# Four feature tiles token-major at the start of the MLPs and the short convolution, in products of 512 columns

## Chip, core and metric

The kernel runs on one core of a Trainium2 chip. The metric is the device time of one execution in microseconds (us). A core has TensorE (PE in the profile, with PEld for its weight loads), VectorE (DVE), ScalarE (ACT), GpSimd (POOL), SyncE (SP, which issues the loads here), an on-chip memory (SBUF) and the accumulators of TensorE (PSUM, eight banks of 512 fp32 columns).

## What is computed

Two blocks of two layers each, on 256 tokens of 1024 features, all in fp32. Each layer has a mixer (two kinds of attention in block 1; a difference attention and a short convolution in block 2) and an MLP of 2816 features. The parts that the change touches, cut from the reference:

```python
# block 1, each layer
h = modulate(rmsnorm(x, g_ffn_pre[i]), sh_f, sc_f)
gate = jnp.einsum('bsd,df->bsf', h, w_ffn_gate[i])
up = jnp.einsum('bsd,df->bsf', h, w_ffn_up[i])
gate = causal_depthwise_conv(gate, w_conv[i], b_conv[i])   # width 3, along the tokens
y = jnp.einsum('bsf,fd->bsd', jax.nn.silu(gate) * up, w_ffn_down[i])
x = x + gt_f[:, None, :] * rmsnorm(y, g_ffn_post[i])
...
# block 2, each layer
g, u = jnp.split(h @ w_gate_up, 2, axis=-1)
return (jax.nn.silu(g) * u) @ w_down
...
# block 2, second mixer
b_gate, c_gate, u = jnp.split(h @ w_in, 3, axis=-1)
return (b_gate * dwconv(c_gate * u, conv_w)) @ w_out
```

## The kernel before

Every fp32 operand of a large product is split into two parts, H and L (`split`, L601: ACT casts H, DVE subtracts to get L), and each product is three matmuls, HH, HL and LH (`mm3`, L611). Weights come in chunks of 1 MB, 128 rows by 2048 columns, loaded in the order of use by SP (`chunk`, L594) and split in two halves of 1024 columns (`Stream.take`, L577): tiles wh and wl. At most 24 wh and wl tiles are alive at a time, that is six chunks, and three unsplit chunks (the SLOTS entry K8).

A stage ends with `tail` (L905): for token tile 0 and then 1 (128 tokens each) it takes the sums acc, updates x, normalises it (tile u), transposes it on PE (tps), scales and shifts it (hf) and splits it into h, feature-major (h0h, h0l for the first four feature tiles, h1h, h1l for the last four). So a token tile's h is complete before the other's.

Five stages start with `first_tiles` (L872): the four MLPs (`ffn`, L1180) and the short convolution (L1488). For the first EARLY = 2 feature tiles it makes both products (gate and up, or c and u) token-major: h of one token tile is the stationary operand, the 256 columns of one feature tile's two matrices are the moving one (tiles fp, in PSUM class "acc"). Token tile 0 is done first, while tile 1's h is made. ACT copies the result to SBUF (fps), and PE transposes it back to feature-major into a bank of class "mm" (fpt). The other 20 tiles of an MLP (6 of the convolution) are made feature-major by `project_t` (L897), with weights stationary and all 256 tokens moving, straight into an "mm" bank (gu; cu and bb in the convolution).

What follows is the same for both kinds: in block 1, t (ACT) and two more steps of t (DVE) make the convolution along the tokens, then s (Silu, ACT), y = s * up (DVE), and y's split into yh (ACT) and yl (DVE). In block 2 s is made straight from the bank. y is the last reader of a tile's bank. PE adds y times w_down to the four sums acc of 512 columns. There are four banks of class "acc" and four of class "mm", each class handed out in turn (L1597).

The order of the instructions is not written by hand. The program is recorded (`Rec`), and a list scheduler (`schedule`, L382) with fixed costs for each operation takes, for an engine that is free, the operation that comes first in the recorded order of those whose operands and buffers are there. Each engine then runs its list strictly in that order.

```python
EARLY = 2
...
def mm3(self, out, a, b, start, stop):
    mm(out, lhsT=a[0], rhs=b[0], start=start, stop=False)
    mm(out, lhsT=a[0], rhs=b[1], start=False, stop=False)
    mm(out, lhsT=a[1], rhs=b[0], start=False, stop=stop)
...
SLOTS = {"S": 64, "K1": 14, "K2": 12, "K4": 32, "K8": 3, "acc": 4, "mm": 4}
```

Of the kernel before, what the change touches and what calls it, by code (L numbers as in the profile page):

```python
# [22 lines left out]
EARLY = 2  # feature tiles at the start of a stage that are made token-major, a token tile at a time  # L23
LASTF, LASTD = 6, 4  # last terms of a sum that run a token tile at a time (the MLPs, the difference attention)
VLAG, QPIECES, WOFROM = 4, 2, 13  # the difference attention's order: values behind weights, the first values, w_o
# [7 lines left out]
# ---------------------------------------------------------------- layout of the inputs  # L33


def vec_layout():
    """Columns of the packed feature-major vectors: name -> (first column, count)."""
# [69 lines left out]
def pack_small(a):  # L107
    """Vectors that every partition reads: lambda's four, the q and k gains and the gains of the
    rotation's partner features."""
# [9 lines left out]
def pack_consts():  # L119
    """Constants of the shapes alone: identity, the two causal masks, head selectors, rope tables."""  # L120
# [18 lines left out]
def pack_chunks(a, plan):  # L139
    out = np.empty((len(plan), P, CH), np.float32)  # L140
    for i, parts in enumerate(plan):
        o = 0
        for name, layer, r0, nr, c0, nc_ in parts:
            w = a[name][layer]
            if r0 is None:  # nr tiles of columns from c0, as rows
# [9 lines left out]
# ---------------------------------------------------------------- recording and ordering of the program  # L155
#
# The program is traced into operations on virtual tiles, list-scheduled on a model of the engines (first
# the operation that comes first in the trace, of those whose operands are there), and emitted in that order.
# [4 lines left out]
AGAIN = {"PE": 0.0, "DVE": 127.0, "ACT": 153.0, "POOL": 100.0, "SP": 0.0}  # from a result to its reader  # L163
# [18 lines left out]
class VAP:  # L182
    """A view of a virtual tile: the partitions, the positions on the free axes, and how to get it from the tile."""
# [79 lines left out]
class Rec:  # L263
    """Takes the place of nc and of the tile pools while the program is traced."""
# [18 lines left out]
    def record(self, eng, fn, args, kw):  # L283
# [16 lines left out]
        if fn == "matmul" and kw["start"]:  # one open group of sums in a bank  # L300
            v = outs[0]
            for w in v.t.writes:
                if w[3] is not op and w[1] < v.parts[1] and w[2] > v.parts[0]:
                    op.deps.setdefault(w[3], 1)
# [31 lines left out]
    def cost(self, op, outs, ins, args, kw):  # L336
        fn = op.fn
        n = int(outs[0].idx.size) if outs else 0
        if op.eng == "PE":
# [4 lines left out]
            side = {32: 4, 64: 2}.get(kw["lhsT"].shape[1], 1)  # tiles of columns that run side by side  # L344
# [1289 lines left out]
```

## Time and profile before

| | |
|---|---|
| time, three runs | 1366.46, 1366.72, 1367.65 us (median 1366.72) |
| span of the profiled execution, first to last instruction | 1366.3 us; no time is on record for what lies around it in that execution, and the median of the runs is 0.4 us above the span |
| busy | PE 1328.7 us (97%), DVE 1082.2 (79%), ACT 718.3 (53%), POOL 112.2 (8%) |
| mean granted TensorE clock | 0.993 |
| matmuls | 8872, each with its weight load |

Matmuls overlap, so the duration of one (0.28 us for 256 columns, 0.39 for 512) is longer than the distance from its start to the next start; the pace is read from start times. Every instruction is put down to L543, since one helper emits them all; operations are told apart by the tiles that they write and read (out<-in). "<-" behind an idle time names what ended it. The four MLPs start at about 154, 482, 876 and 1171 us, the short convolution at about 1070 us (first fp products).

### The profile page before, as it was taken

The numbers are of one execution on the slowest core, as the hardware profiler recorded it, in microseconds if no ns is written. First come the engines' busy times: TensorE is split into PE (matmuls) and PEld (weight loads), VectorE is DVE, ScalarE is ACT, GpSimd is POOL, SyncE is SP. The second block draws the span as 40 slices with busy tenths as digits, with TensorE's granted clock in tenths as the row PEclk, the third lists the DMA queues.
The fourth block names the chain that finished last, engine by engine and source line by source line (L and its number), as shares of the span: only waits on it lengthen the run. The fifth ranks groups of instructions, "written<-read, shape, count | busy, mean of one in ns | idle before, by whom it ended". The sixth has DMA issues, their size and how long they took to land.

```text
span 1366.3 us, 22283 instructions
## 1 busy us (share of the span) xinstructions
PE 1328.7 (97%) x8872; PEld 1193.9 (87%) x8872; DVE 1082.2 (79%) x1807; ACT 718.3 (53%) x1273; POOL 112.2 (8%) x168
## 2 busy tenths in 40 slices
PE   5899999999999999999999999999999999899998
PEld 3788799999888799999888888799999899899997
DVE  6888988998988499999799977877777898755542
ACT  3565665555666474557444566754444535644430
POOL 1000200000200010101143122300000100100000
PEclk9999999999999999999999999999999999999999
DMA  9857578887676156777554541577776688355520
GB/s 360 307 213 272 192 296 324 316 325 304 228 248 262 48 186 272 277 251 261 194 185 167 189 150 63 185 270 291 274 278 254 235 304 313 140 200 185 185 94 31
DMA packets 45320, 311.84 MB, mean 228 GB/s; under 512 B 5280, under 2 KB 5664, under 8 KB 8864
## 3 DMA queue, kind: packets, MB, share of 16 engines
q1 hardware_dynamic: 45216, 310.42, 61.3%
q8 instruction: 69, 1.13, 0.3%
q14 instruction: 35, 0.29, 0.1%
HBM read 309.35 MB, written 1.05 MB: 227 GB/s over the span
## 4 chain that ended last, share of the span: by engine, by line
PE 89%; DVE 4%; ACT 2%; POOL 2%; issue 2%; DMA 0%; SPq 0%; POOLq 0%; ACTq 0%
PE gu L543 34%; PE acc L543 29%; PE qkps L543 7%; PE fp L543 4%; PE cu L543 3%; PE z L543 2%; PE dz L543 2%; PE bb L543 2%; PE qps L543 2%; PE op L543 1%; DVE w L543 1%; ACT junk L543 1%; POOL sst L543 1%; PE kc L543 1%; DVE u L543 1%
## 5 line engine op out<-in xcount | busy, mean ns | idle before, releaser
L543 DVE TENSOR_TENSOR wl<-w,wh 128x1024 fp32r<-128x1024 f32 x392 | 471.3, 1220 | 82.8 <-ACT wh L543 59.7
L543 ACT CAST wh<-w 128x1024 fp32r<-128x1024 f32 x392 | 402.7, 1049 | 98.2 <-DMA w<-in_wst_dram 67.8
L543 DVE CUSTOM_DVE_ANT_0 w<-w,rows,vec 128x1024 f32<-128x1024 f32 x192 | 242.3, 1278 | 15.3 <-DMA w<-in_wst_dram 15.1
L543 PE MATMUL gu<-h1h,wl 128*128 128x256 f32 x640 | 181.4, 284 | 0.0
L543 PE MATMUL gu<-h1h,wh 128*128 128x256 f32 x640 | 181.3, 283 | 0.0
L543 PE MATMUL gu<-h0l,wh 128*128 128x256 f32 x640 | 181.3, 283 | 0.0
L543 PE MATMUL gu<-h1l,wh 128*128 128x256 f32 x640 | 181.3, 283 | 0.0
L543 PE MATMUL gu<-h0h,wl 128*128 128x256 f32 x640 | 181.3, 283 | 0.0
L543 PE MATMUL gu<-h0h,wh 128*128 128x256 f32 x640 | 181.2, 283 | 0.0
L543 PE MATMUL acc<-wh,yh 128*128 128x512 f32 x352 | 137.8, 392 | 0.7 <-ACT yh L543 0.7
L543 PE MATMUL acc<-wl,yh 128*128 128x512 f32 x352 | 137.7, 392 | 0.0
L543 PE MATMUL acc<-wh,yl 128*128 128x512 f32 x352 | 136.1, 389 | 0.0
L543 PEld LDWEIGHTS gu<-h0h,wh 128*128 128x128 f32 x640 | 122.6, 192 | 2.3
L543 PEld LDWEIGHTS gu<-h0l,wh 128*128 128x128 f32 x640 | 122.7, 192 | 2.2
L543 PEld LDWEIGHTS gu<-h1h,wh 128*128 128x128 f32 x640 | 123.0, 192 | 0.1
L543 PEld LDWEIGHTS gu<-h1l,wh 128*128 128x128 f32 x640 | 122.9, 192 | 0.0
L543 PEld LDWEIGHTS gu<-h1h,wl 128*128 128x128 f32 x640 | 122.9, 192 | 0.0
L543 PEld LDWEIGHTS gu<-h0h,wl 128*128 128x128 f32 x640 | 122.7, 192 | 0.1
L543 DVE TENSOR_TENSOR y<-s,gu 128x256 f32<-128x256 f32 x80 | 33.4, 418 | 73.1 <-ACT s L543 73.1
L543 ACT ACTIVATE s<-gu 128x256 f32<-128x256 f32 x40 | 15.4, 384 | 136.5 <-PE gu L543 136.5
L543 POOL TENSOR_SCALAR sst<-ss 128x1 f32<-128x1 f32 x26 | 25.7, 987 | 734.5 <-ACT junk L543 734.2
L543 PEld LDWEIGHTS acc<-wh,yl 128*128 128x128 f32 x352 | 66.1, 188 | 14.2
(358 smaller groups left out, 2834.1 us busy)
## 6 DMA issues: line engine op xcount, KB each, us to landing
w<-in_wst_dram SPq DMA_DIRECT2D x284, 1024.0 KB, 4.8
w<-in_wst_dram SPq DMA_DIRECT2D x16, 512.0 KB, 11.4
x<-in_x_dram SPq DMA_DIRECT2D x2, 512.0 KB, 6.5
cx<-in_ctx_dram SPq DMA_DIRECT2D x2, 512.0 KB, 6.0
out_dram<-x SPq DMA_DIRECT2D x1, 512.0 KB, 2.6
out_dram<-x SPq DMA_DIRECT2D x2, 256.0 KB, 2.0
cst<-in_consts_dram SPq DMA_DIRECT2D x1, 264.0 KB, 5.1
smalls<-in_smalls_dram SPq DMA_DIRECT2D x1, 256.0 KB, 6.7
```

The source lines that it names most:

```text
L543: fn(*[real(a) for a in op.args], **{k: real(v) for k, v in op.kw.items()})
```

## The change

EARLY goes from 2 to 4. The early tiles are made two at a time: the chunks of a pair hold, for each row tile, the columns of both tiles' two matrices side by side (512 columns), two chunks to a pair (`pair_specs` in place of `both_spec`). `first_tiles` takes the chunks of both pairs first, then makes for each token tile and pair one bank fp of 512 columns with 24 products of 512, and copies it. The transposes are as before, for four tiles. The remaining 18 tiles of an MLP (4 of the convolution, whose bb tiles are unchanged) stay feature-major. The number of chunks is unchanged. Comments and docstrings are removed as well, which changes line numbers alone.

```diff
-EARLY = 2
+EARLY = 4
...
     @staticmethod
-    def both_spec(a, b):
-        return tuple((n, i, k * P, 1, c, P) for k in range(KT) for n, i, c in (a, b))
+    def pair_specs(tiles):
+        return [
+            tuple((n, i, k * P, 1, c, P) for k in range(g * 4, g * 4 + 4) for t in tiles for n, i, c in t) for g in range(2)
+        ]
 
     def first_tiles(self, ht, n):
         nc = self.nc
-        ws = [self.w.take() for f in range(n)]
+        ws = [sum((self.w.take() for g in range(2)), []) for p in range(n // 2)]
         out = {}
         for t in range(2):
-            for f in range(n):
-                if f % 2 == 0:
-                    ps = self.pacc.tile([P, 512], F32, tag="acc", name="fp")
-                    out[t, f // 2] = self.sb.tile([P, 512], F32, name="fps")
-                o = f % 2 * S
+            for p in range(n // 2):
+                ps = self.pacc.tile([P, 512], F32, tag="acc", name="fp")
                 for kt in range(KT):
-                    w = [z[:, kt % 4 * S : (kt % 4 + 1) * S] for z in ws[f][kt // 4]]
-                    self.mm3(ps[:, o : o + S], self.hx(ht, t, kt), w, kt == 0, kt == KT - 1)
-                if f % 2 == 1 or f == n - 1:
-                    nc.scalar.copy(out[t, f // 2][:, 0 : o + S], ps[:, 0 : o + S])
+                    w = [z[:, kt % 2 * 512 : (kt % 2 + 1) * 512] for z in ws[p][kt // 2]]
+                    self.mm3(ps, self.hx(ht, t, kt), w, kt == 0, kt == KT - 1)
+                out[t, p] = self.sb.tile([P, 512], F32, name="fps")
+                nc.scalar.copy(out[t, p], ps)
...
         tiles = [[(n, i, c + f * P) for n, c in ab] for f in range(NF)]
-        return [self.both_spec(*x) if f < EARLY else tuple((n, i, 0, 8, c, P) for n, i, c in x) for f, x in enumerate(tiles)]
+        out = []
+        for f in range(0, EARLY, 2):
+            out += self.pair_specs(tiles[f : f + 2])
+        return out + [tuple((n, i, 0, 8, c, P) for n, i, c in x) for x in tiles[EARLY:]]
...
-        out = [self.both_spec(cols(1, f), cols(2, f)) for f in range(EARLY)]
+        out = []
+        for f in range(0, EARLY, 2):
+            out += self.pair_specs([(cols(1, f + k), cols(2, f + k)) for k in range(2)])
```

The scheduler makes a new order of it. The first place is PE in the first MLP, behind the last token-major products of token tile 1 (fp_1688 before). fpt_1714 and fpt_1718 are the transposed tiles 0 and 1, gu_1777 and gu_1856 the products of tiles 2 and 3; "waits" names whose progress the instruction waits for. Before:

```order
L543 MATMUL fp_1688<-wh_1612,h1h_1587 128x256
L543 MATMUL fp_1688<-wl_1622,h1h_1587 128x256
L543 MATMUL fp_1688<-wh_1612,h1l_1594 128x256
L543 MATMUL gu_1777<-h0h_1569,wh_1709 128x256 [waits Activation_49]
L543 MATMUL gu_1777<-h0l_1577,wh_1709 128x256
L543 MATMUL gu_1777<-h0h_1569,wl_1725 128x256 [waits DVE_49]
```

And now, where fp_1758 is token tile 1's second pair, fpt_1805, 1810, 1819 and 1824 are the transposed tiles 0 to 3, and gu_1858 is tile 4:

```order
L543 MATMUL fp_1758<-wh_1699,h1l_1593 128x512
L543 MATMUL fpt_1805<-eye_85,fps_1706 128x128 [waits Activation_49]
L543 MATMUL fpt_1805<-eye_85,fps_1762 128x128 [waits Activation_49]
...
L543 MATMUL fpt_1810<-eye_85,fps_1762 128x128
L543 MATMUL fpt_1819<-eye_85,fps_1735 128x128 x2
L543 MATMUL fpt_1824<-eye_85,fps_1735 128x128 x2
L543 MATMUL fpt_1819<-eye_85,fps_1812 128x128 [waits Activation_49]
L543 MATMUL fpt_1819<-eye_85,fps_1812 128x128
L543 MATMUL fpt_1824<-eye_85,fps_1812 128x128 x2
L543 MATMUL gu_1858<-h0h_1569,wh_1767 128x256 [waits DVE_49]
```

Where gu products followed the token-major ones before, all sixteen transposes follow now. gu_1858 is the fifth tile in the four "mm" banks from fpt_1805 on, and the DVE step that it waits for is y_1850, of tile 0.

The second place is DVE in the same MLP, the steps between the last subtractions of weights and y. Before (t_365 and t_380 are tiles 0 and 1):

```order
L543 TENSOR_TENSOR wl_1803<-w_400_1712,wh_1787 128x1024 [waits DMAHW0_49,Activation_49]
L543 SCALAR_TENSOR_TENSOR t_365_1799<-fpt_1714,vec_90,t_365_1799 128x255 [waits Activation_49]
L543 SCALAR_TENSOR_TENSOR t_365_1799<-fpt_1714,vec_90,t_365_1799 128x254 [waits DVE_49]
L543 SCALAR_TENSOR_TENSOR t_380_1808<-fpt_1718,vec_90,t_380_1808 128x255 [waits Activation_49]
L543 SCALAR_TENSOR_TENSOR t_380_1808<-fpt_1718,vec_90,t_380_1808 128x254 [waits DVE_49]
L543 TENSOR_TENSOR wl_1840<-w_400_1712,wh_1814 128x1024 [waits Activation_49]
L543 TENSOR_TENSOR y_1854<-s_1831,fpt_1714 128x256 [waits Activation_49]
```

And now (t_379, t_394, t_400 and t_411 are tiles 0 to 3):

```order
L543 TENSOR_TENSOR wl_1800<-w_426_1743,wh_1791 128x1024 [waits DMAHW2_49,PE_49,Activation_49]
L543 TENSOR_TENSOR wl_1816<-w_426_1743,wh_1802 128x1024 [waits PE_49,Activation_49]
L543 SCALAR_TENSOR_TENSOR t_379_1822<-fpt_1805,vec_90,t_379_1822 128x255 [waits Activation_49]
L543 SCALAR_TENSOR_TENSOR t_379_1822<-fpt_1805,vec_90,t_379_1822 128x254 [waits DVE_49]
L543 SCALAR_TENSOR_TENSOR t_394_1829<-fpt_1810,vec_90,t_394_1829 128x255 [waits Activation_49]
L543 SCALAR_TENSOR_TENSOR t_394_1829<-fpt_1810,vec_90,t_394_1829 128x254 [waits DVE_49]
L543 SCALAR_TENSOR_TENSOR t_400_1834<-fpt_1819,vec_90,t_400_1834 128x255 [waits Activation_49]
L543 SCALAR_TENSOR_TENSOR t_400_1834<-fpt_1819,vec_90,t_400_1834 128x254 [waits DVE_49]
L543 SCALAR_TENSOR_TENSOR t_411_1839<-fpt_1824,vec_90,t_411_1839 128x255 [waits Activation_49]
L543 TENSOR_TENSOR y_1850<-s_1842,fpt_1805 128x256 [waits Activation_49]
```

Seven steps of t stand ahead of the first y, four of them before. On ACT the last copy fps, the four t, the load of the Silu table and three s follow each other in that order, where before two t, a cast, the table load and two s did. In the second MLP the three engines have the same order there; in the third there are no t, and the table load stands between the last copy and the first s; in the fourth no table is loaded. In the short convolution the 48 products bb of tiles 0 and 1 stand between the transposes of tiles 1 and 2.

## Rows read from the trace of the kernel before

**Rows 1.** The page: busy time of each engine, and the shares of the chain that ended last, by engine.

```profile
PE 1328.7 (97%) x8872; PEld 1193.9 (87%) x8872; DVE 1082.2 (79%) x1807; ACT 718.3 (53%) x1273; POOL 112.2 (8%) x168
...
PE 89%; DVE 4%; ACT 2%; POOL 2%; issue 2%; DMA 0%; SPq 0%; POOLq 0%; ACTq 0%
```

**Rows 2.** Who waited for whom, PE's waits: waiting tile and what it waited for, us in total, times, longest.

```profile
PE tps L543 <- DVE u L543: 6.1, 6, 2.7
PE fp L543 <- ACT h0h L543: 4.2, 8, 0.8
...
PE fpt L543 <- ACT fps L543: 0.3, 1, 0.3
```

**Rows 3.** PE's timeline in the middle of the first MLP: start us, us, engine, line, operation, shape. Between the first two rows stand 47 more products of 256 columns (gu), between the last two 11 more of 512 (acc).

```profile
199.92 0.28 PE L543 MATMUL gu<-h0h,wh 128*128 128x256 f32 x1
...
205.67 0.40 PE L543 MATMUL acc<-wh,yh 128*128 128x512 f32 x1
...
208.42 0.28 PE L543 MATMUL gu<-h0h,wh 128*128 128x256 f32 x1
```

**Rows 4.** PE's timeline at the end of the first MLP's token-major products: the first gu product, the four transposes of a tile, the product behind them.

```profile
171.26 0.28 PE L543 MATMUL gu<-h0h,wh 128*128 128x256 f32 x1
...
172.34 0.60 PE L543 MATMUL fpt<-eye,fps 128*128 128x128 f32 x4
172.70 0.36 PE L543 MATMUL gu<-h0h,wh 128*128 128x256 f32 x1
```

**Rows 5.** PE's timeline, rows with idle time ahead of them (in brackets, with what ended it) at the starts of the first, second and third MLP and of the short convolution.

```profile
152.65 1.06 PE L543 MATMUL tps<-eye,u 128*128 128x128 f32 x8 [1.73 <-DVE u L543]
...
165.16 0.39 PE L543 MATMUL fp<-wh,h0h 128*128 128x256 f32 x1 [0.33 <-ACT h0h L543]
...
165.95 0.66 PE L543 MATMUL fpt<-eye,fps 128*128 128x128 f32 x4 [0.28 <-ACT fps L543]
...
491.59 0.39 PE L543 MATMUL fp<-wh,h0h 128*128 128x256 f32 x1 [0.31 <-ACT h0h L543]
...
883.40 1.06 PE L543 MATMUL tps<-eye,u 128*128 128x128 f32 x8 [0.52 <-DVE u L543]
...
1071.11 0.38 PE L543 MATMUL fp<-wh,h0h 128*128 128x256 f32 x1 [0.24 <-ACT h0h L543]
...
1071.85 0.39 PE L543 MATMUL fp<-wh,h0l 128*128 128x256 f32 x1 [0.24 <-DVE h0l L543]
...
1076.34 1.09 PE L543 MATMUL tps<-eye,u 128*128 128x128 f32 x8 [0.16 <-DVE u L543]
...
1078.59 0.39 PE L543 MATMUL fp<-wh,h0h 128*128 128x256 f32 x1 [0.45 <-ACT h0h L543]
```

**Rows 6.** Timeline of ACT, then of DVE, from the last copy fps of the first MLP to the first y.

```profile
171.46 0.59 ACT L543 COPY fps<-fp 128x512 f32<-128x512 f32 x1 [1.76 <-PE fp L543]
171.94 1.05 ACT L543 CAST wh<-w 128x1024 fp32r<-128x1024 f32 x1
172.89 1.02 ACT L543 ACTIVATE t<-fpt,vec 128x256 f32<-128x256 f32 x2
...
175.24 1.28 ACT L543 ACT_TABLE_LOAD   x1 [0.39 <-DVE t L543]
176.53 0.73 ACT L543 ACTIVATE s<-t 128x256 f32<-128x256 f32 x2
...
174.17 1.90 DVE L543 SCALAR_TENSOR_TENSOR t<-fpt,vec,t 128x255 f32<-128x255 f32 x4
...
177.12 0.74 DVE L543 TENSOR_TENSOR y<-s,fpt 128x256 f32<-128x256 f32 x2
```

**Rows 7.** ACT's timeline at the same place of the third MLP.

```profile
893.80 0.58 ACT L543 COPY fps<-fp 128x512 f32<-128x512 f32 x1 [0.51 <-PE fp L543]
894.40 1.28 ACT L543 ACT_TABLE_LOAD   x1
895.93 0.66 ACT L543 ACTIVATE s<-fpt 128x256 f32<-128x256 f32 x2 [0.25 <-PE fpt L543]
```

**Rows 8.** Stretches: from and to, length, then busy us (and instructions) of PE, PEld, DVE, ACT and POOL, the granted TensorE clock, the DMA share, GB/s.

```profile
30.90:34.30 3.40, 1.74 (x8) 1.12 (x6) 3.40 (x8) 1.05 (x1) 0.00 (x0) 1.00 1.02 408
34.30:37.70 3.40, 2.44 (x11) 2.03 (x12) 3.40 (x6) 1.94 (x4) 0.00 (x0) 1.00 1.05 426
...
147.00:153.80 6.80, 4.99 (x26) 3.78 (x24) 6.53 (x11) 4.91 (x12) 4.05 (x7) 1.00 0.52 195
153.80:160.60 6.80, 6.15 (x28) 6.07 (x29) 5.97 (x13) 6.80 (x16) 3.48 (x3) 0.50 0.22 94
...
874.00:877.40 3.40, 1.91 (x12) 1.44 (x13) 3.31 (x10) 2.20 (x8) 0.06 (x1) 1.00 0.86 308
877.40:880.80 3.40, 3.40 (x18) 3.36 (x17) 3.40 (x7) 3.40 (x10) 1.80 (x1) 0.50 0.01 2
...
1167.60:1171.00 3.40, 1.24 (x9) 1.03 (x10) 2.94 (x9) 1.85 (x7) 1.07 (x3) 1.00 0.00 0
1171.00:1174.40 3.40, 3.38 (x14) 3.00 (x15) 2.94 (x8) 3.23 (x8) 2.68 (x1) 0.50 0.00 0
```

**Rows 9.** Groups of instructions on ACT and on DVE, the split of weights: count, busy us and mean ns of one, idle time before them and what ended it.

```profile
L543 ACT CAST wh<-w 128x1024 fp32r<-128x1024 f32 x392 | 402.7, 1049 | 98.2 <-DMA w<-in_wst_dram 67.8 <-PE gu L543 17.7 <-PE acc L543 5.4
L543 DVE TENSOR_TENSOR wl<-w,wh 128x1024 fp32r<-128x1024 f32 x392 | 471.3, 1220 | 82.8 <-ACT wh L543 59.7 <-PE gu L543 11.5 <-issue 10.5
```

## The prediction

> **What bounds the kernel now.** I read the page first: PE is busy for 1328.7 of the 1366.3 us span, and 89% of the chain that ended last lies on PE [rows 1]. So time is won or lost only where PE does its products at another pace or stands idle. Next I read PE's waits by releaser. Apart from the load phase at the start, the entries that touch this change are the waits of the transposes for u, of the first products for h, and a short one for their copy: 6.1, 4.2 and 0.3 us [rows 2]. The reader should see that almost nothing is idle in the middle of a stage. The trace before shows no wait of the first gu product for a bank.
>
> Then I read PE's timeline for the pace, because the durations of overlapping products say nothing about it. From 199.92 to 205.67 us, 48 products of 256 columns start, 0.1198 us apart; the next 12, of 512 columns, take 2.75 us, 0.2292 us apart [rows 3]. Four transposes stand 0.36 us before the next product, so one is 0.09 us [rows 4].
>
> **The change, part by part.** All sums are made against the profiled execution, whose span is 1366.3 us. The median of the runs shown is 1366.72 us, so I add 0.4 us at the end.
>
> *Products.* In each of five stages (four MLPs, the short convolution) the first four feature tiles took 96 token-major products of 256 columns for tiles 0 and 1 and 96 feature-major ones of 256 for tiles 2 and 3: 192 x 0.1198 = 23.0 us. Now they are 96 products of 512: 96 x 0.2292 = 22.0 us. That is -1.0 us a stage and -5.0 us in all. The Trainium skill, "TensorE: Matmul & The Clock Gate", section Back-to-back issue gap, gives a fixed cost of 2.5 ns for each product on top of its columns; by that 96 fewer products would save 0.24 us a stage, 1.2 us in all, and the forecast would be 3.8 us later. The rows decide, and they show 10.4 ns for each pair of products made one.
>
> *Transposes.* Tiles 2 and 3 now have to be turned too: 8 more in a stage, 8 x 0.09 = 0.72 us, in all +3.6 us, on PE and hidden by nothing. The two more copies from PSUM a stage lie on ACT (53% busy) beside PE's work; the last of them is in the chain below.
>
> *Weights.* The number of chunks is unchanged, and so are their loads, casts and subtractions (1049 and 1220 ns each [rows 9]). Four chunks instead of two must be split when a stage starts, but token tile 0 also has 48 x 0.2292 = 11.0 us of products in place of 5.75, and PE's new order puts products of token tile 1 with the first pair wherever the second pair's halves are due. I cost this at nothing; without that cover it is one subtraction, 1.2 us, for each stage.
>
> *Waits that go.* Inside the starts PE waited for token tile 1's h, or for its transposes' input, or for the copy: 0.33 and 0.28 us in the first MLP, 0.31 in the second, 0.52 in the third, and 0.24, 0.24, 0.16 and 0.45 in the convolution, 2.5 us together [rows 5]. A piece of h now feeds three products of 0.2292, 0.69 us in place of 0.36, and a second pair can fill in, so most go: I take -2.0 us (bounds 0 and -2.5). The wait for token tile 0 (1.73 us at 152.65 [rows 5]) stays: nothing new can run before the first h.
>
> *The new wait.* The transposed tiles go to the four "mm" banks. Before, tiles 0 and 1 took two and the gu products of tiles 2 and 3 used the others, so PE had 96 products to do while ACT and DVE worked on tiles 0 and 1. Now four transposed tiles fill all four banks, and the first gu product (tile 4) waits on DVE: for y of tile 0, the last reader of its bank. Behind it on PE stand all of gu and the first acc products; nothing overtakes. The length, with T the moment at which PE goes from the products to the transposes: the copy starts 0.20 us after T (171.26 to 171.46 [rows 4, 6]) and takes 0.59, to 0.79. PE does its 16 transposes meanwhile and, at T + 1.5, is out of work. In the first two MLPs the chain on ACT and DVE is: t of tile 0 from 0.68 (the step from copy to next is 0.48) for 0.56, to 1.24; then on DVE seven steps of t before y, 0.475 each (four in 1.90 us), from about 1.4 to 4.7. Meanwhile ACT does the other three t at steps of 0.46, to 2.6, loads its table (1.28), to 3.9, and makes s (0.42), to 4.3 [rows 6]. So y runs from 4.7 to 5.1, and PE goes on at about 5.3. That is an idle stretch of 3.8; I take 3.7 us, twice. In the third MLP there is no convolution, but there is the table load: copy to 0.79, table to 2.1, s 0.36 to 2.5, y to 3.1 [rows 6, 7], PE at 3.2: 1.7 us. In the fourth no table is loaded: s to 1.2, y to 1.8, PE at 1.9: 0.4 us. In the short convolution the bb products stand between the transposes of tiles 1 and 2 and take the third bank at once: 0. Together +9.5 us (bounds 6 if every hand-over is as short as it can be, 12 if DVE still has one subtraction to do ahead of the t steps).
>
> *The clock.* Where PE stood idle at a stage start, the granted clock fell to 0.50, 1.2 GHz, soon after: it was busy 4.99 of 6.80 us before the fall at 153.8 (6.8 us long), 1.91 of 3.40 before the one at 877.4, and 1.24 of 3.40 before the one at 1171; but with 1.74 of 3.40 at 30.9 it stayed at 1.00 [rows 8]. A fall of 3.4 us costs 1.7 us of products. The two waits of 3.7 us, with 1.5 us of short transposes ahead of them, are as idle as the stretch at 1167.6, so I expect a fall after each: +3.4 us. The wait of 1.7 us is like the one at 874, as likely to bring a fall as not; I leave it out of the sum and in the range. The Trainium skill, same page, section A second HAM failure mode: psum-queue depth-cycling, says that cycling through PSUM banks makes PE idle briefly between groups of products so often that its clock goes back and forth. This speaks against the change; the trace agrees as far as it shows a fall after short idle stretches, and shows none yet that a bank caused.
>
> The sum: -5.0 + 3.6 - 2.0 + 9.5 + 3.4 = +9.5 us; 1366.3 + 9.5 + 0.4 = **1376.2 us**.
>
> **The rivals.**
> - *The waits come, the clock holds*: +6.1 us, 1372.8. For it: the stretch at 30.9, idle for half of its time without a fall. Against it: the falls after three of the five tails. If the waits are at their lower bound too, it is 1369.3.
> - *The second pair's weights are late* as well: 1.2 us for each of five stages, 1382. For it: ACT and DVE do their splitting in order with the tail, and the wait for the copy at 165.95 shows that ACT is full there. Against it: PE's order fills these places with other products.
> - *The wider products win*, the other side: the banks come free in time because the chain from copy to y is passed faster than its rows say, and what is left is -5.0 + 3.6 - 2.0 = -3.4 us, 1363.3. The place is the first gu product of each MLP; it decides for faster from an average wait below 0.85 us (3.4 over four stages), with no fall of the clock. For it: before, the same chain never held PE up. Against it: then gu products covered it, and the table load alone is 1.28 us.
> - *The change doesn't do what it says* (the 512-column products run at the pace of two of 256): the sum is 5.0 us later, 1381.2. The acc rows, with the same shape and the same kind of operands, speak against it.
>
> **How the numbers follow.** Forecast 0.58; clock holds 0.19; late weights 0.09; wider products win 0.09; no gain in pace 0.05. What a measurement of this kernel can tell from no change is about 0.2%, 2.7 us: faster is below 1364.0, slower above 1369.4. Faster has 0.05 (half of its rival), within 0.2% 0.09 (the other half, and the lowest part of the case in which the clock holds), slower 0.86. The range goes from 1369 (short waits, clock held) to 1382 (a third fall, or a second stretch at half clock as at 153.8, with no wait gone); the forecast's own is 1374 to 1379.
>
> **What would show it.** In PE's waits a new entry, gu on DVE y, four times: about 3.7, 3.7, 1.7 and 0.4 us. The fp products still 480, but of 512 columns and 0.229 us apart, gu 576 a group in place of 640, and 80 transposes fpt in place of 40. In the clock's rows two stretches at 0.50 soon after the first gu product of the first two MLPs. On ACT the table load after four t, with PE idle beside it. I am wrong if PE's timeline shows no idle time ahead of gu, if that idle time is under 1 us, or if fp waits for weights (wh, wl) for more than 2 us in all.

## The result, and the profile after

The changed kernel takes 1375.18 us (median of four runs) where the kernel before takes 1366.72 beside it (median of three): the ratio is 1.006, with a 95% interval from 1.0048 to 1.0072. It is slower, 8.5 us by the medians, and 1 us below the 1376.2 that was predicted. One more run of the kernel before (1839 us) and the profiled run of acc_banks below (1845 us) fell into a much slower state of the chip, and no figure of this document uses them. The profiled execution took 1374.88 us with a span of 1373.1, which is 6.8 us more than the span before. In the runs on record the time is 1.7 to 2.2 us above the span, so the profiled execution before, with its span of 1366.3, was itself some 1.3 us above its median, and the spans differ by less than the medians.

The page of the changed kernel, busy time and the chain by engine, against [rows 1]:

```profile
PE 1326.3 (97%) x8432; PEld 1169.1 (85%) x8432; DVE 1083.3 (79%) x1807; ACT 724.1 (53%) x1283; POOL 110.1 (8%) x168
...
PE 81%; DVE 9%; ACT 3%; POOL 3%; issue 2%; DMA 2%; SPq 0%; POOLq 0%; ACTq 0%; DVEq 0%
```

PE's busy time hardly moved. The chain tells more: PE's share went from 89% to 81%, DVE's from 4% to 9%. The same work now more often waits for DVE. PE's waits (waiting tile, what it waited for, us in total, times, longest), against [rows 2]:

```profile
PE gu L543 <- DVE y L543: 7.8, 4, 3.1
...
PE tps L543 <- DVE u L543: 7.1, 7, 2.5
...
PE fp L543 <- ACT h0h L543: 3.2, 5, 0.8
PE acc L543 <- ACT yh L543: 2.8, 3, 1.4
...
PE fp L543 <- DVE wl L543: 0.5, 1, 0.5
```

The first entry is the new wait that was predicted. The entry of acc was not: before, acc waited once for yh, 0.7 us; now it waits three times, 2.8 us. The timelines at the end of the first MLP's token-major products (start, us, engine, operation, shape, idle time before; compare [rows 4, 6]). PE's:

```profile
177.22 0.39 PE L543 MATMUL fp<-wh,h1l 128*128 128x512 f32 x1
177.45 1.91 PE L543 MATMUL fpt<-eye,fps 128*128 128x128 f32 x16
182.43 0.58 PE L543 MATMUL gu<-h0h,wh 128*128 128x256 f32 x1 [3.08 <-DVE y L543]
```

ACT's, from the last copy to s:

```profile
177.70 0.59 ACT L543 COPY fps<-fp 128x512 f32<-128x512 f32 x1 [1.12 <-PE fp L543]
178.18 2.01 ACT L543 ACTIVATE t<-fpt,vec 128x256 f32<-128x256 f32 x4
180.21 1.28 ACT L543 ACT_TABLE_LOAD   x1
181.51 1.03 ACT L543 ACTIVATE s<-t 128x256 f32<-128x256 f32 x3
```

DVE's, the t steps and y:

```profile
178.79 3.21 DVE L543 SCALAR_TENSOR_TENSOR t<-fpt,vec,t 128x255 f32<-128x255 f32 x7 [0.39 <-ACT t L543]
181.96 1.08 DVE L543 TENSOR_TENSOR y<-s,fpt 128x256 f32<-128x256 f32 x3
```

From the first transpose to the first gu product pass 4.98 us; the prediction's chain gave 5.3. The table load and the seven t steps run side by side, and y starts at 181.96, when both s (0.42 after 181.51) and the t steps have just ended.

Where the time came from is best seen by stage, each from its first fp product in PE's timeline to the next stage's (the last to PE's last instruction), in us:

| stretch | before | after |
|---|---|---|
| start to first MLP | 154.4 | 152.7 |
| first MLP and second attention | 327.6 | 330.0 |
| second MLP and difference attention | 394.4 | 403.3 |
| third MLP | 193.1 | 192.2 |
| short convolution | 101.2 | 100.0 |
| fourth MLP | 190.5 | 189.9 |

Three stretches with the change are faster, and most of the loss is in that of the second MLP: 8.9 us, of which the new wait is 3.1. The clock has a part in the others: before, 6.8 us of the first MLP and 3.4 of the third ran at half clock [rows 8], and in the changed kernel 3.4 of the first MLP alone. That alone takes 1.7 us off each of the two stretches, more than the whole gain of the third MLP. The second MLP's stretch has no half clock in either kernel. The 1.7 us ahead of the first MLP need not be the change's: before_rows below, whose edit stands behind that place, takes 153.0 there.

### The profile page after: what moved, and what is told of

Its sections match the earlier page's. It is cut to its first block, busy times and chain, and to the rows that moved or that the text cites. A ratio compares the mean times of both kernels' runs of the same rounds, so it can differ in the third digit from the quotient of the medians.

```text
span 1373.1 us, 21420 instructions
## 1 busy us (share of the span) xinstructions
PE 1326.3 (97%) x8432; PEld 1169.1 (85%) x8432; DVE 1083.3 (79%) x1807; ACT 724.1 (53%) x1283; POOL 110.1 (8%) x168
## 4 chain that ended last, share of the span: by engine, by line
PE 81%; DVE 9%; ACT 3%; POOL 3%; issue 2%; DMA 2%; SPq 0%; POOLq 0%; ACTq 0%; DVEq 0%
PE gu L543 27%; PE acc L543 27%; PE qkps L543 7%; PE fp L543 6%; DVE w L543 3%; PE z L543 2%; DVE wl L543 2%; PE dz L543 2%; PE cu L543 2%; PE qps L543 2%; DMA w<-in_wst_dram 1%; PE op L543 1%; DVE djunk L543 1%; PE bb L543 1%; POOL sst L543 1%
## 5 line engine op out<-in xcount | busy, mean ns | idle before, releaser
L543 PE MATMUL gu<-h0h,wh 128*128 128x256 f32 x576 | 164.1, 285 | 8.0 <-DVE y L543 7.8
L543 PE MATMUL gu<-h0h,wl 128*128 128x256 f32 x576 | 163.8, 284 | 0.2 <-DVE wl L543 0.2
L543 PE MATMUL gu<-h0l,wh 128*128 128x256 f32 x576 | 163.5, 284 | 0.0
L543 PE MATMUL gu<-h1h,wh 128*128 128x256 f32 x576 | 163.1, 283 | 0.0
L543 PE MATMUL gu<-h1l,wh 128*128 128x256 f32 x576 | 163.0, 283 | 0.0
L543 PE MATMUL gu<-h1h,wl 128*128 128x256 f32 x576 | 163.0, 283 | 0.0
L543 PEld LDWEIGHTS gu<-h1h,wh 128*128 128x128 f32 x576 | 110.7, 192 | 0.1
L543 PEld LDWEIGHTS gu<-h1l,wh 128*128 128x128 f32 x576 | 110.6, 192 | 0.0
L543 PEld LDWEIGHTS gu<-h1h,wl 128*128 128x128 f32 x576 | 110.5, 192 | 0.1
L543 PEld LDWEIGHTS acc<-wh,yh 128*128 128x128 f32 x352 | 66.3, 188 | 15.6 <-ACT yh L543 3.6
```

The source lines that it names most:

```text
L543: fn(*[real(a) for a in op.args], **{k: real(v) for k, v in op.kw.items()})
```

## The experiments

All times are medians, beside the kernel before on the same chip. Where kernels that stand beside different times of the kernel before are compared, the difference is good to about 1 us: its medians go from 1366.7 to 1367.9.

| kernel | time | before | ratio, 95% interval |
|---|---|---|---|
| two_wide | 1368.74 | 1367.72 | 1.0007, 0.9998 to 1.0016 |
| four_narrow | 1383.37 | 1367.72 | 1.0116, 1.0102 to 1.0130 |
| acc_banks | 1367.39 | 1367.72 | 0.9996, 0.9987 to 1.0005 |
| gu_between | 1370.76 | 1367.72 | 1.0019, 1.0010 to 1.0028 |
| after_rows | 1371.38 | 1367.62 | 1.0025, 1.0014 to 1.0036 |
| before_rows | 1366.00 | 1367.62 | 0.9991, 0.9982 to 1.0000 |
| two_wide_rows | 1361.49 | 1367.62 | 0.9958, 0.9945 to 0.9970 |
| acc_banks_rows | 1363.55 | 1367.62 | 0.9972, 0.9961 to 0.9983 |
| rows_late | 1379.09 | 1367.93 | 1.0083, 1.0070 to 1.0097 |
| silu_first | 1366.94 | 1367.93 | 0.9996, 0.9987 to 1.0004 |
| gu_between_rows | 1364.16 | 1367.93 | 0.9972, 0.9962 to 0.9983 |
| mixed_rows | 1358.75 | 1367.93 | 0.9934, 0.9921 to 0.9948 |

### Width, tiles and banks apart

**two_wide** is the changed kernel with one pair, **four_narrow** the kernel before with four tiles.

```diff
-EARLY = 4
+EARLY = 2
```

> Two early feature tiles as before, but as one pair in products of 512 columns: width alone, without the two more transposed tiles and without a full set of mm banks. My theory (the banks cost, the width gains): fp is 48 products of 512 a stage at 0.229 us in place of 96 of 256 at 0.120, so -0.5 us a stage and -2.5 us in all against the kernel before, with at most 1 us of the small waits inside the starts gone besides; no wait of gu for y; 1363.5 to 1365.5 us where the kernel before has 1367.2. Rival (width gains nothing, all that the changed kernel shows comes from the order): within 0.5 us of the kernel before. Second rival (fp of a pair needs two chunks split before it ends, and these come late): fp waits for wh or wl by 1 us or more a stage, slower than before by 3 us or more.

It came out at 1368.7, 1.0 above before: neither the gain of the width nor the rival's nothing, and no late weights (one wait of fp for wl, 0.5 us). By stage the first, third and fourth MLP, the convolution and the start took 5.0 us less than before, the second MLP with the difference attention 6.9 more, though no gu waits for a bank there at the start. The 5.0 can't be read as the width's: the 10.2 us at half clock at 153.8 and 877.4 us of the kernel before [rows 8] are not in this execution, and they alone are 5.1 us of products. The 6.9 holds, since neither kernel has half clock there. So something in the second MLP is lost without the banks.

```diff
-EARLY = 2  # feature tiles at the start of a stage that are made token-major, a token tile at a time
+EARLY = 4  # feature tiles at the start of a stage that are made token-major, a token tile at a time
```

> Four early feature tiles, but each in products of 256 columns as before: the banks and transposes of the changed kernel without its width. My theory: the new wait of gu for y stays as in the changed kernel (3.1, 3.1, 1.1 us at the starts of the first three MLPs), and the products cost 1.0 us more a stage, so 5 us more than the changed kernel: 1379 to 1381 us. Rival (the width gains nothing): 1374 to 1376. If the order around the second MLP is what costs the changed kernel most (its waits for yh and weights in the middle, 3.4 us), it can go either way by some 3 us here, and the waits of that MLP must then differ from the changed kernel's while the new waits stay.

1383.4, above the expected range: 8.2 us more than the changed kernel, 7.2 when each is set against the kernel before beside it. That is more than the 5.0 of the sum, but not the width alone: waits differ too. The new wait is 3.0, 1.5 and 1.1 us in the first three MLPs; in the second the transposes had waited 1.0 us before for ACT's copy of rows (on rows, see below), and one gu waits 1.5 us for wl. The pace of fp is read from PE's timeline in the second MLP. In four_narrow 84 products lie from the first row to the second:

```profile
499.88 0.28 PE L543 MATMUL fp<-wh,h0l 128*128 128x256 f32 x1
...
509.96 0.28 PE L543 MATMUL fp<-wh,h1l 128*128 128x256 f32 x1
```

In the changed kernel 49:

```profile
494.74 0.39 PE L543 MATMUL fp<-wl,h1h 128*128 128x512 f32 x1
...
505.84 0.39 PE L543 MATMUL fp<-wh,h1l 128*128 128x512 f32 x1
```

That is 0.1200 us against 0.2265: 13.5 ns for each pair of products made one, 1.3 us a stage, 6.5 in all.

**acc_banks** and **gu_between** both free the bank on which the first gu waits.

```diff
+            pool = self.pmm if f < 2 else self.pacc
-            ps = self.pmm.tile([P, 512], F32, tag="mm", name="fpt")
+            ps = pool.tile([P, 512], F32, tag="mm", name="fpt")
```

> The changed kernel with the transposed tiles 2 and 3 in two of the acc banks, so that two mm banks are free for the gu products of tiles 4 and 5. My theory (the banks cost): the wait of the first gu for y goes at all four MLPs (7.8 us in the changed kernel); instead the first acc product, 20 to 44 gu products later, waits for the y of tiles 2 and 3, which leave the acc banks: at most 2 us in each of the first two MLPs and nothing in the others, so 1368 to 1372 us. The fall of the clock after the first MLP's wait need not come, 1.7 us less. Rival (the wait is for the work of ACT and DVE on the four tiles and only moves to acc): the waits move to acc in full and the time stays within 1.5 us of the changed kernel's 1375.2. Second rival (the second MLP's waits for yh and weights, 3.4 us, have a cause of their own): these stay whatever the bank does.

1367.4, level with before, 7.8 below the changed kernel and 0.6 under the expected range. By the time, the wait did not move in full, and the theory of the banks holds. Its waits are not read here, so the second rival is left to the next kernel; those of the same banks with early rows stand under acc_banks_rows.

```diff
+        fs = [0, 1, 4, 5, 2, 3] + list(range(6, NF))
-        wd = Stream(self, [((name, i, f * P, 2, 0, D),) for f in range(0, NF, 2)])
+        wd = Stream(self, [((name, i, f * P, 2, 0, D),) for f in fs[::2]])
...
-        for f in range(NF + 1):
+        for n in range(NF + 1):
+            f = fs[n] if n < NF else NF
...
-            j = f - 1
+            j = fs[n - 1] if n else -1
...
-                self.bg(max(0, (f - 3) / (NF - 4)))
+                self.bg(max(0, (n - 3) / (NF - 4)))
```

> The changed kernel with the gu products of tiles 4 and 5 put, in the MLPs, between the transposes of tiles 0, 1 and those of tiles 2, 3, so that the banks are shared out as before: two transposed tiles, two of gu. My theory (the banks cost): 48 or more gu products (5.8 us) cover the chain from copy to y, the wait of gu for y goes at all four MLPs (7.8 us) and no other takes its place, so 1365.5 to 1368.5 us, the kernel before's time; without the fall of the clock after it 1.7 us less. Rival (the wait only moves, since ACT and DVE have the same four tiles to do at the start): waits of acc for yh or of fpt for banks of 1 us and more in the first two MLPs, 1371 us or more. Second rival (the waits in the middle of the second MLP have a cause of their own, DVE's background work or the weights): these stay at 2 us or more while the wait for the bank goes.

1370.8, between the theory's range and the first rival's. Its trace speaks for the second rival: no wait for the bank at an MLP's start, and in the middle of the second MLP (482 to 632 us, PE's waits) this:

```profile
PE acc L543 <- ACT yh L543: 4.4, 3, 3.0
PE gu L543 <- DVE y L543: 0.6, 1, 0.6
```

### What is lost in the second MLP

So the second MLP was read again. Stretches of the kernel before (length, then busy us of PE, PEld, DVE, ACT, POOL, the granted clock, DMA share, GB/s):

```profile
500.00:520.00 20.00, 20.00 (x137) 18.55 (x137) 19.08 (x35) 10.17 (x18) 0.00 (x0) 1.00 0.53 202
520.00:540.00 20.00, 20.00 (x148) 19.02 (x147) 19.73 (x27) 10.49 (x15) 0.00 (x0) 1.00 0.77 297
540.00:560.00 20.00, 20.00 (x140) 18.65 (x139) 18.13 (x30) 8.46 (x13) 0.00 (x0) 1.00 0.62 232
```

The same of the changed kernel:

```profile
500.00:520.00 20.00, 16.92 (x90) 14.36 (x89) 11.10 (x21) 10.87 (x19) 0.00 (x0) 1.00 0.43 157
520.00:540.00 20.00, 20.00 (x144) 18.76 (x143) 13.29 (x22) 6.41 (x12) 0.00 (x0) 1.00 0.26 97
540.00:560.00 20.00, 18.47 (x130) 16.77 (x129) 18.62 (x28) 8.57 (x12) 0.00 (x0) 1.00 0.72 275
560.00:580.00 20.00, 19.28 (x137) 17.77 (x137) 19.89 (x33) 11.63 (x22) 6.72 (x6) 1.00 0.77 286
580.00:600.00 20.00, 19.08 (x135) 17.55 (x134) 19.89 (x32) 9.69 (x14) 0.00 (x0) 1.00 0.76 290
```

Before, DVE works almost without a break from 500 us on. After, it is idle for 15.6 of the 40 us from 500 to 540, the loads fall to 97 GB/s, and then DVE is full (19.89 of 20) while PE has holes. What DVE does there beside the MLP's own steps is background work of the difference attention's modulation (djunk, w): products of loaded chunks with two tiles rows, which PE makes by 16 transposes rowps of cact into "mm" banks and ACT copies. In the kernel before, ACT's timeline has the last copies of rows here:

```profile
493.71 1.10 ACT L543 COPY rows<-rowps 128x512 f32<-128x512 f32 x2
```

and DVE's the first djunk, which waits only for its chunk:

```profile
500.15 1.28 DVE L543 CUSTOM_DVE_ANT_0 djunk<-w,rows,vec 128x1024 bf16<-128x1024 f32 x1 [0.86 <-DMA w<-in_wst_dram]
```

In the changed kernel PE's timeline has the transposes here:

```profile
527.84 1.91 PE L543 MATMUL rowps<-eye,cact 128*128 128x128 f32 x16
```

DVE's has the first djunk:

```profile
531.28 1.28 DVE L543 CUSTOM_DVE_ANT_0 djunk<-w,rows,vec 128x1024 bf16<-128x1024 f32 x1 [0.72 <-ACT rows L543]
```

and between 523 and 537 us SP's queue waited for one thing:

```profile
SPq L543 <- DVE msh_a L543: 14.4, 1, 14.4
```

Before, those transposes stood between the first token-major products of the stage, 482.7 to 491.3 us, in PE's timeline from

```profile
482.71 0.54 PE L543 MATMUL rowps<-eye,cact 128*128 128x128 f32 x3
...
490.46 0.82 PE L543 MATMUL rowps<-eye,cact 128*128 128x128 f32 x6
```

where the changed kernel has wide products. After, PE makes them at 527.8, behind the gu products of tile 4 and 48 acc products. The first two chunks of the background work were loaded all the same, at 492.5 and 501.6 us, in the order recorded. There are three buffers for unsplit chunks (K8 in SLOTS); two of them held these chunks until rows was there, so every weight chunk had to pass through the third. The next load, of the third background chunk, stood 14.4 us in SP's queue until DVE was done with the first, and the weights behind it stood too. In two_wide 12 of the 16 transposes are early, but the last copy of rows is at 526.06 us, and the first djunk at 527.5.

**after_rows, before_rows, two_wide_rows, acc_banks_rows** record the two rows tiles ahead of the second MLP, so that PE makes them first thing; nothing else differs from the kernel in their name.

```diff
+        for k in (1, 2):
+            self.cb[k] = self.on_all_rows(self.cact[:, k * 8 : k * 8 + 8])
+
         def units():
-            for k in (1, 2):
-                self.cb[k] = self.on_all_rows(self.cact[:, k * 8 : k * 8 + 8])
             yield from self.mod_units(1, 0, MODS[:2])
```

> The changed kernel with one edit: the two rows tiles (the conditions, spread over all partitions by 16 transposes into mm banks) that the second MLP's background work on DVE reads are recorded ahead of that MLP instead of inside it. My new theory: the changed kernel makes rows 40 us later than the kernel before (531 us against 490), and until then two and then all three of the unsplit-chunk buffers hold chunks of that background work, so weight loads stand (from 521.7 to 536.5 us none is issued) and DVE, idle first, is late afterwards: this, not the banks, made some 6 us of the changed kernel's 8. Then the waits for yh and weights in the middle of the second MLP (3.7 us) go, second MLP and difference attention take about 397 us in place of 403, and the time is 1368.5 to 1370.5 us. Rival (the waits there come from the bank wait having put gu and acc out of step): no change in that MLP beyond 1 us, 1374 to 1376.

1371.4, 3.8 below the changed kernel (0.9 above the expected range). In its second MLP the waits for yh and for weights are gone; the wait for the bank grew from 3.1 to 4.0, and 3.4 us at half clock follow it (the last row of this document). These two, 0.9 and 1.7 us, are why the stretch took 399.1 and not 397. PE's waits there, 482 to 632 us:

```profile
PE gu L543 <- DVE y L543: 4.0, 1, 4.0
PE fp L543 <- ACT h0h L543: 0.6, 1, 0.6
```

And DVE (the third busy time) is full again where the changed kernel's was idle:

```profile
500.00:520.00 20.00, 15.99 (x75) 13.36 (x74) 19.55 (x35) 13.04 (x21) 0.00 (x0) 0.91 0.56 201
520.00:540.00 20.00, 20.00 (x132) 18.42 (x131) 17.97 (x26) 7.78 (x11) 0.00 (x0) 1.00 0.66 247
```

> The kernel before with the same edit (rows recorded ahead of the second MLP): there PE makes rows at the start of the MLP anyhow, in gaps of 480 to 491 us. New theory: within 1 us of the kernel before, 1367 to 1368.5. Rival (making rows early is a gain of its own that has nothing to do with the change): faster than before by 2 us or more.

1366.0, a gain of 1.6 whose interval reaches to no gain: 1.0 better than expected and short of the rival's 2. The edit gives the others 3.8 to 7.2, so most of that is the late rows; up to 1.6 of it may be a gain that the edit has in any case.

> One pair of 512 columns (two early tiles) with rows recorded ahead of the second MLP. Without that edit it was 1368.7, no faster than before, though its first, third and fourth MLP and the convolution together took 5 us less in the trace and the second MLP with the difference attention 6.9 us more. New theory (late rows hid the gain of the width): the second MLP's loss goes, 1362.5 to 1365 us, faster than the kernel before by 0.2% or more. Rival (the second MLP loses because the pair itself asks for its weights in another order): 1367 us or more.

1361.5, 7.2 less than two_wide, faster than before and 1 us under the expected range. The second MLP with the difference attention takes 393.5 us in place of 401.3. The width had gained all along, and late rows had hidden it.

> Four early tiles in pairs, tiles 2 and 3 transposed into acc banks, and rows recorded ahead of the second MLP: both causes taken away. Without the second edit it was 1367.7. If the two causes add (bank waits 7.2 us, late rows some 6), 1361 to 1363.5 us, and no wait of gu for y or of acc for yh above 0.5 us in the first two MLPs. If they are the same loss seen twice (DVE and ACT have the early tiles to do in any case), 1366 to 1368.

1363.55, at the upper end: the causes add. Against after_rows the banks are worth 7.8, against acc_banks the rows 3.8. PE's waits over the first two MLPs (152 to 632 us) name no y and no yh:

```profile
PE fp L543 <- ACT h0h L543: 1.3, 2, 0.7
PE tps L543 <- DVE u L543: 0.7, 1, 0.7
PE fp L543 <- DVE wl L543: 0.6, 1, 0.6
PE acc L543 <- ACT h0h L543: 0.3, 1, 0.3
```

### The cause put in by hand, the chain, and the best of both

**rows_late** is the kernel before with one small DVE operation ahead of the rows:

```diff
+                self.lasty = y
...
+            late = self.sb.tile([P, 16], F32, name="late")
+            self.nc.vector.scalar_tensor_tensor(
+                out=late, in0=self.lasty[:, 0:16], scalar=0.0, in1=self.cact[:, 8:24], op0=ALU.mult, op1=ALU.add
+            )
             for k in (1, 2):
-                self.cb[k] = self.on_all_rows(self.cact[:, k * 8 : k * 8 + 8])
+                self.cb[k] = self.on_all_rows(late[:, k * 8 - 8 : k * 8])
```

> The kernel before, made to have its rows late: the 16 columns from which the two rows tiles are made pass first through one small DVE operation that adds zero times y of tile 4, so that PE cannot make rows before that y (some 43 us into the second MLP); bit for bit the same values, nothing else changed. My theory (chunks of the background work that wait for rows hold the unsplit-chunk buffers, so weight loads stand and DVE is late afterwards): a stretch of 10 us or more without a load between 500 and 530 us, waits of acc for yh in the middle of the second MLP, 3 to 8 us slower than the kernel before, 1370.5 to 1375.5. Rival (the second MLP loses time only when four early tiles or a pair change the order of the weights): within 1.5 us of the kernel before.

1379.1, 11.2 us slower, more than expected (3 to 8). Late rows alone, without any wide product or full set of banks, cost more than the whole change. Stretches of this kernel:

```profile
500.00:520.00 20.00, 20.00 (x137) 18.55 (x136) 10.83 (x20) 10.47 (x18) 0.00 (x0) 1.00 0.38 142
520.00:540.00 20.00, 20.00 (x149) 18.98 (x148) 10.66 (x19) 5.99 (x11) 0.00 (x0) 1.00 0.32 109
```

Its longest entry of PE's waits from 482 to 632 us:

```profile
PE acc L543 <- ACT yh L543: 4.5, 3, 1.9
```

The picture is that of the changed kernel, stronger: DVE idle for 18.5 of 40 us, the first djunk at 533.74.

**silu_first** is after_rows with the table loaded earlier.

```diff
-    def first_tiles(self, ht, n):
+    def first_tiles(self, ht, n, silu=False):
...
                 nc.scalar.copy(out[t, p], ps)
+                if silu and t == 0 and p == n // 2 - 1:
+                    first = self.sb.tile([P, 1], F32, name="first")
+                    nc.scalar.activation(out=first, in_=out[t, p][:, 0:1], func=AF.Silu)
...
-        early = self.first_tiles(self.h, EARLY)
+        early = self.first_tiles(self.h, EARLY, True)
```

> The changed kernel with rows early, and with ACT's table load for Silu moved out of the chain from copy to y: a Silu of one column of token tile 0's last copy, whose result nobody reads, loads the table 11 us earlier, beside the products of token tile 1. My theory (the wait for the bank is the length of the chain copy, t, table load, s, y): the wait of the first gu falls from 3.1 to about 1.9 us in the first MLP, from 4.0 to about 2.9 in the second (a cast stands ahead of s there), and from 1.1 to 0 in the third; 3 to 3.5 us less than without it (1371.4), 1367.5 to 1369. Rival (DVE's seven t steps alone set the end, since they end with the table load): the waits of the first two MLPs stay within 0.3 us, only the third's goes, 1370 to 1371.

1366.9, 4.4 below after_rows and a little under the range. The waits are 2.4, 2.7 and none. In the first MLP the scheduler now puts y behind four t steps in place of seven; there the wait is 0.5 longer than expected, since DVE is at a subtraction of weights until 179.3 us, 0.8 after ACT's first t. The chain sets the length of the wait, and DVE's part of it as well as ACT's.

**gu_between_rows** is gu_between with early rows.

> Four early tiles with the gu products of tiles 4 and 5 between the transposes of tiles 0, 1 and 2, 3, and rows recorded ahead of the second MLP. Without the latter it was 1370.8, with a wait of 3.0 us of acc for yh in the second MLP. If that wait was the late rows' doing: it goes with the others there, and the time is 1362 to 1365 us, like the kernel with two acc banks (1363.6). If it was the early tiles' work on ACT and DVE, moved: a wait of 2 us or more for yh or a bank stays within 50 us of the second MLP's start, 1366 to 1369.

1364.2: the wait of 3.0 for yh was late rows. **mixed_rows** takes acc_banks_rows and makes only one pair in the second, third and fourth MLP.

```diff
-        for f in range(0, EARLY, 2):
+        n = 4 if (b, i) == (0, 0) else 2
+        for f in range(0, n, 2):
...
-        early = self.first_tiles(self.h, EARLY)
+        n = 4 if (b, i) == (0, 0) else 2
+        early = self.first_tiles(self.h, n)
```

> The stages' best of the traces so far put together, with rows recorded ahead of the second MLP: four early tiles with two of them in acc banks in the first MLP and the convolution, one pair in the other three MLPs. In the traces the first MLP is 1.5 us shorter with four (325.1 against 326.6) and the convolution 1.7 us (99.1 against 100.8), the second MLP with the difference attention 3.2 us shorter with two (393.5 against 396.7) and the third MLP 1.4 (190.7 against 192.1). If stages add up: 1358 to 1360 us, below one pair in all stages (1361.5). If the loss of a stage comes with what the stage before it leaves (the wait of 4.1 us for u at the third MLP's start with four): 1361 to 1364.

1358.75: 9.2 us, 0.66%, faster than before, and the best of all kernels here. Its stretches take 152.3, 325.1, 393.5, 192.1, 99.6 and 190.7 us; the third MLP did not show the 190.7 that was counted on.

## Why the prediction was right, and where it was not

The time and the sign came out, and the new wait is of the kind and in the place that was forecast. That the number came out within 1 us is luck in part: two terms were too large and one cause was missing, and these nearly cancel. By the runs the 8.5 us are +7.8 from the banks (after_rows against acc_banks_rows), +3.8 from late rows (the changed kernel against after_rows), and -3.1 for all the rest; acc_banks_rows against the kernel before beside it gives -4.1 for that rest. The prediction had +12.9 from the banks (9.5 of waits and 3.4 of clock), nothing, and -3.4.

- **Products, -5.0.** Mis-sized: -6.5 by the pace of fp; the 7.2 to 8.2 by four_narrow hold other waits as well. The rows that were taken [rows 3] were gu and acc; fp at 512 columns is a little faster than acc (0.2265 against 0.2292). The rows show 13.5 ns for each product that falls away. The Trainium skill, "TensorE: Matmul & The Clock Gate", section Back-to-back issue gap, gives 2.5 ns, in a formula that leaves out the load of weights; with a load for each product, as here, the trace doesn't agree.
- **Transposes, +3.6.** Mis-sized. The sixteen take 1.91 us in the three MLPs where PE then waits, 1.7 in the fourth and 1.6 in the convolution, and the eight took 0.6 to 0.8 (starts in PE's timeline): +5.4 in all. The 0.09 of four transposes with a product behind them [rows 4] doesn't hold for sixteen: 0.10 each with a product behind them, 0.12 with nothing behind.
- **Weights, 0.** Right at the starts: fp waits for wl once, 0.5 us. The weights that came late were those of the second MLP's middle, and not for the reason given to the rival.
- **Waits that go, -2.0.** The step that failed. The waits inside the starts fell from 2.5 [rows 5] to 1.7 us only. And the step asked what a second pair would put into the gaps between the first products, not what stood there already: in the second MLP before, PE had made rows there, and it now makes them 40 us later. The prediction has no term for that; it is the 3.8 us of late rows.
- **The new wait, +9.5.** Right in kind and place, a little long: 3.08, 3.08, 1.09 and none, against 3.7, 3.7, 1.7 and 0.4; of the four waits that the profile counts, the fourth is another, 0.56 us later in the second MLP. The chain was 0.3 shorter than worked out, and the transposes before it 0.4 longer.
- **The clock, +3.4.** Half borne out. Stretches of the changed kernel, with the granted clock as the last but two column: the first MLP's wait and what follows, then the second's.

```profile
177.45:181.90 4.45, 1.91 (x17) 1.67 (x15) 3.95 (x8) 4.17 (x8) 0.00 (x0) 1.00 0.94 379
181.94:185.35 3.41, 2.92 (x13) 2.92 (x14) 3.41 (x10) 2.77 (x7) 0.00 (x0) 0.50 0.21 89
...
506.07:511.00 4.93, 1.91 (x17) 1.67 (x15) 4.08 (x10) 4.68 (x9) 0.00 (x0) 1.00 0.01 3
511.06:514.50 3.44, 3.44 (x22) 3.15 (x23) 3.36 (x8) 2.28 (x6) 0.00 (x0) 1.00 0.12 19
```

After the first wait the clock fell to 0.50 (1.2 GHz) for 3.4 us, after the second it stayed at 1.00 (2.4 GHz). At the same time the 6.8 us at 153.8 and the 3.4 us at 877.4 [rows 8] were not there any more. From the first MLP to the last product, half clock is 6.8 us after and 13.6 before, which is 3.4 us of products gained, not lost, in this execution. That gain is not shown to be the change's: the 6.8 us at 153.8 are not in the traces of before_rows and rows_late either, which are the kernel before up to there, and the mean granted clock of the changed kernel's four runs goes from 0.990 to 0.997. What the Trainium skill says under A second HAM failure mode: psum-queue depth-cycling, on the same page, is borne out by the one wait for a bank and not by the other.

By terms the profiled executions give -6.5 + 5.4 - 0.8 + 7.2 - 3.4, with 3.1 for the waits in the middle of the second MLP and 0.8 for a longer wait for u at the third MLP's start: +5.8 of the 6.8. The rest, with the 1.7 by which the stretch ahead of the first MLP was shorter, is not explained.

Open are three things: whether rows came late because PE had no gap for them or because the "mm" banks were full, which no run separates (in two_wide, with two transposed tiles in place of four, 4 of the 16 were still late); where the 1.6 us of before_rows come from; and the wait of 4.1 us for u at the third MLP's start in acc_banks_rows and gu_between_rows (1.6 in after_rows).

## What to carry to other kernels

A change that fills an engine's gaps can move whatever the scheduler had put there; look up what stood there, and follow it to its readers, before a gap is counted as time won. Work that is loaded ahead in order holds its buffers until its last operand is there: one small late operand, 16 transposes here, can hold up a whole weight stream, and the cost shows tens of us later, on another engine. When a buffer class is filled to the last by a new kind of tile, the price is the chain from its first writer to its last reader less what the engine still has to do; order other work between, borrow buffers of another class, or shorten the chain.

## What the runs showed of the hardware

The granted clock fell behind the wait for a bank in the first MLP in each of the four traces that have it (waits of 3.08 us in the changed kernel and in after_rows, 3.02 in four_narrow, 2.38 in silu_first), and between 165 and 200 us it stayed at 1.00 in nine traces without it. But the fall is not settled by PE's idle time alone. PE was busy 1.91 of 4.45 us ahead of the fall at 181.9 us and 1.91 of 4.93 ahead of 511.1 without one; in after_rows, where the second MLP's wait is 4.0 us, this row of the stretch behind it shows the fall:

```profile
513.83:517.24 3.41, 3.32 (x10) 2.88 (x11) 3.28 (x9) 3.41 (x8) 0.00 (x0) 0.50 0.00 0
```

And a product of 512 columns costs 0.2265 us where two of 256 cost 0.2400. With two early tiles, where the width brings no transposes with it, that is 48 x 13.5 ns x 5 = 3.2 us; two_wide_rows is 4.5 us below before_rows. An estimate of what the clock adds: the mean granted clock of their runs is 0.9964 against 0.9955, and 0.0009 of 1361 us is 1.2 us.
